# Compressed branch of the decode sequences: two sequences per pass, 256 columns for each weight block

## Chip, core and metric

One core of a Trainium2 chip runs the whole program. The metric is the device time in microseconds of one execution. Engines are named as the profile names them: PE (matmul, with its weight loads as PEld), DVE (vector), ACT (scalar), POOL, and SP, which here only issues DMAs.

## What is computed

One step of a small decoder trunk: a conformer layer (depthwise convolution and a SwiGLU feed-forward) and then a sparse-attention layer, for a prompt of 512 tokens and for 8 decode sequences of 4 tokens with a cache of 1024 tokens each. The part that is changed is the compressed branch of the 8 decode sequences. Each block of 32 cached tokens becomes one key and one value for each of 4 heads, by a two-layer network on the 32*64 = 2048 numbers of the block:

```python
def compress(kv_full, w_phi1, b_phi1, w_phi2, b_phi2, pe_cmp):
    blk = kv_full[:, :n * CMP_BLOCK].reshape(B, n, CMP_BLOCK, 2, KV_HEADS, HEAD_DIM)
    blk = blk + pe_cmp.transpose(1, 0, 2)[:, :, None, :]
    blk = blk.transpose(0, 1, 3, 4, 2, 5).reshape(B, n, 2, KV_HEADS, CMP_BLOCK * HEAD_DIM)
    hid = jax.nn.silu(jnp.einsum('bnegf,efh->bnegh', blk, w_phi1) + b_phi1[:, None, :])
    out = jnp.einsum('bnegh,ehd->bnegd', hid, w_phi2) + b_phi2[:, None, :]
```

A sequence has 32 blocks and 4 heads, so 128 columns for keys (e = 0) and 128 for values (e = 1). The cache is float32 and these products are made in plain float32; `w_phi1` has 16 blocks of 128x128 for each e. The embedding `pe_cmp` is the same for all blocks, so its share is worked out once and added to the bias.

## The kernel before, in words

A scheduler sets the order on each engine: the program is written as nested Python generators, each instruction gets a priority by its place in the code, and inside `tc.high_priority(-LATER)` it gets a lower one, so that it fills places where an engine would wait. The instructions of one engine then run strictly in that order, each waiting for its inputs and for free buffers.

`compress_steps` (lines 1033 to 1071) is such a filler. For each of the 8 sequences b, and for two halves hp, one indirect DMA on POOL (L1030) gathers 1 MB of cache rows into `nat` (2 buffers); DVE transposes it (L1043, two per `nat`) into `xt`, shared by both halves (3 buffers); then for e = 0 and 1 PE multiplies 16 weight blocks `w1`, each 128x128 and stationary, with 128 columns of `xt` into one PSUM bank (L1049). For b = 0 the embedding's share is made between them: the same 16 weight blocks stationary, one column of `peT` moving (L1053), added to the bias on DVE (`bh`, L1055). ACT makes the Silu (`hk`, L1057, 2 buffers), PE the second layer (L1060 for keys, L1066 for values), and DVE adds its bias (`cks`, L1064; `cv`, L1069, one buffer, written to DRAM by L1070). The banks are those of the pool `t`, of which there are two.

The steps are written ahead of the depthwise convolution's end, the layer norm and the second pointwise product of layer 0 (`depthwise`, `layer_norm_out`: L812 are the norm's sums, L818 to L830 its vector work, `h_lo` of L830 its last output, L183 and L185 the large products in fp32r). They are followed by the first feed-forward (`ffn`): eight plain units of gate and up products, of which each ends with one `a_lo` (L920) on POOL, then eight down products, then units with seven half-size products (L247). Beside the feed-forward run the bias tables (L1085 to L1119) and 24 key steps, which gather cache rows (`kr`, L1030), transpose them on DVE (`ktr`, L1304) and write them back to DRAM (L1299, L1307). The bias tables' memory is free only when the compressed branch is done. L452 are the modulation products, a second filler, whose 0.5 MB slabs come through SP's queue with the weights.

Of the kernel before, what the change touches and what calls it, by code (L numbers as in the profile page):

```python
# [7 lines left out]
F32 = mybir.dt.float32  # L8
F32R = mybir.dt.float32r
I32 = mybir.dt.int32  # L10
AF = mybir.ActivationFunctionType
ALU = mybir.AluOpType
AX = mybir.AxisListType

P = 128
# [3 lines left out]
NB = 8  # L19
# [6 lines left out]
G = 4  # L26
R = 4
HD = 64
# [22 lines left out]
STATE = 2  # L51
LAST = KT - 1
ORDER = (0, 1, 2, 3, 4, 5, 6, 7)
MID = 24
PE_CONV = (3, 4, 5, 6, 7)

BUCKET_START = [16, 21, 27, 35, 46, 59, 77, 99, 128, 166, 216, 280, 363, 470, 609, 790]
# [56 lines left out]
class Kernel:  # L114
# [881 lines left out]
    def compress_loads(self, pool):  # L996
        A = self.A

        self.w1 = pool.tile([P, 2, 8, 2, P], F32, name="w1")
        src = A["w_phi1"].rearrange("e (a s h i) n -> e h a i s n", s=8, a=4, h=2)  # L1000
        for e in range(2):
            for h in range(2):
                for a in range(4):
                    self.sy.dma_start(self.w1[32 * a:32 * a + 32, e, :, h], src[e, h, a])
        cp = self.cp
        self.w2k = cp.tile([P, P], F32, name="w2k")
        self.w2v = cp.tile([P, HD], F32, name="w2v")
        for d in range(2):
            self.sy.dma_start(self.w2k[:, d * HD:(d + 1) * HD], A["w_phi2"][0])
        self.sy.dma_start(self.w2v, A["w_phi2"][1])  # L1010
        self.b2k = cp.tile([P, 1], F32, name="b2k")
        b2 = A["b_phi2"][0].rearrange("(d o) -> d o", o=1)
        for d in range(2):
            self.sy.dma_start(self.b2k[d * HD:(d + 1) * HD], b2)
        self.b2v = cp.tile([P, HD], F32, name="b2v")
        self.sy.dma_start(self.b2v, A["b_phi2"][1].rearrange("(o d) -> o d", o=1).broadcast_to([P, HD]))
        self.bh = cp.tile([P, 2], F32, name="bh")
        pe = pool.tile([P, P], F32, name="hk", bufs=2)[:, :HD]
        self.v.memset(pe, 0.0)
        src = A["pe_cmp"].rearrange("e (a s) d -> a e s d", a=4)  # L1020
        for a in range(4):
            for e in range(2):
                self.sy.dma_start(pe[32 * a + 8 * e:32 * a + 8 * e + 8], src[a, e])
        self.peT = pool.tile([P, 2, 32], F32, name="peT")
        self.v.transpose(self.peT, pe.rearrange("p (h i) -> p h i", h=2))
# [6 lines left out]
    def compress_steps(self, pool):  # L1032


        v, s, g, te = self.v, self.s, self.g, self.te
        self.compress_loads(pool)
        for b in range(NB):
            xts = [self.shift_pool.tile([P, 8, 8, 32], F32, name="xt", bufs=3) for _ in range(2)]
            for hp in range(2):
                nat = pool.tile([P, 4, 512], F32, name="nat", bufs=2)  # L1040
                self.load_rows(nat.rearrange("p t e -> p (t e)"), self.A["cache_kv_cmp"], hp, b)
                for e in range(2):
                    v.transpose(xts[e][:, hp * 4:hp * 4 + 4].rearrange("p s q n -> p s (q n)"), nat[:, :, e * 256:(e + 1) * 256])  # L1043
                yield
            for e in range(2):
                xv = xts[e].rearrange("p s (g h) n -> p h s g n", h=2)
                ph = self.bank()
                for c in range(16):
                    te.matmul(ph[:, :P], self.w1[:, e, c // 2, c % 2], xv[:, c % 2, c // 2], start=c == 0, stop=c == 15)  # L1049
                if b == 0:  # L1050
                    pb = self.bank()
                    for c in range(16):
                        te.matmul(pb[:, :1], self.w1[:, e, c // 2, c % 2], self.peT[:, c % 2, e * 8 + c // 2:e * 8 + c // 2 + 1],  # L1053
                                  start=c == 0, stop=c == 15)
                    v.tensor_scalar(self.bh[:, e:e + 1], pb[:, :1], self.b_phi1[:, e:e + 1], None, op0=ALU.add)  # L1055
                hk = pool.tile([P, P], F32, name="hk", bufs=2)
                s.activation(hk, ph[:, :P], AF.Silu, bias=self.bh[:, e:e + 1])  # L1057
                po = self.bank()
                if e == 0:
                    te.matmul(po[:, :P], self.w2k, hk, start=True, stop=True)  # L1060
                    pv = po[:, :P].rearrange("p (q g n) -> p q g n", q=2, g=2)
                    for g2 in range(2):
                        sl = slice(g2 * HD, (g2 + 1) * HD)
                        v.tensor_scalar(self.cks[sl, b], pv[sl, :, g2], self.b2k[sl], None, op0=ALU.add)  # L1064
                else:
                    te.matmul(po[:, :HD], hk, self.w2v, start=True, stop=True)  # L1066
                    cv = pool.tile([32, 256], F32, name="cv", bufs=1)
                    for gg in range(G):
                        v.tensor_tensor(out=cv[:, gg * HD:(gg + 1) * HD], in0=po[gg * 32:(gg + 1) * 32, :HD], in1=self.b2v[:32], op=ALU.add)  # L1069
                    g.dma_start(self.vtail[b, 0:32], cv)  # L1070
            yield
        self.dump("cks", self.cks)

# [572 lines left out]
    def run(self):  # L1646
        tc, A = self.tc, self.A

        def sbuf(name, side="left"):
            return tc.tile_pool(name=name, bufs=1, side=side, reuse_waits="tile")  # L1650

        with sbuf("const") as self.cp, sbuf("norm") as self.np, \
# [17 lines left out]
            with sbuf("conv") as pool:  # L1670
                self.ys0 = pool.tile([P, KT, NS], F32, name="ys0")
                self.conv_pool = pool
                shifting = sbuf("shift", "right")
                self.shift_pool = shifting.__enter__()
                with sbuf("setup", "right") as sp:
                    self.setup(sp)
                    between = self.ada_steps(0, 2)
                    ada1 = itertools.chain(*(self.ada_steps(1, part) for part in (1, 0, 2)))
                    units_ = self.gated_units(pool, between)
                    next(units_)  # L1680
                    self.state_parts(sp)
                compressing = sbuf("compress", "right")
                self.compress_pool = compressing.__enter__()
                next(units_)
                compress = self.compress_steps(self.compress_pool)

                with tc.high_priority(-LATER):
                    for _ in between:
                        pass
                    for _ in range(MID):  # L1690
                        next(compress)
                acc = self.depthwise(pool)
                with tc.high_priority(-LATER):
                    self.conv_states(pool)
                self.layer_norm_out(pool, acc, ada1)
# [119 lines left out]
```

## Time and profile before

| | |
|---|---|
| median of 3 runs (range) | 1661.1 us (1657.52 to 1663.83) |
| profiled execution: time, span of its instructions | 1661.26 us, 1659.5 us |
| busy: PE, DVE, ACT, POOL | 1555.0, 1107.8, 694.1, 235.2 us |
| mean granted clock of TensorE | 0.975 |
| DMA | 295.26 MB, mean 178 GB/s |

The profiled execution's span lies 1.8 us under its own time, and that time 0.2 us over the median. Busy time says little about matmuls, because consecutive ones overlap: what one costs is the distance from its start to the next one's. A float32 matmul shows as two records. The granted clock is given in shares of 2.4 GHz: 1.00 is that level, 0.50 is 1.2 GHz.

### The profile page before, as it was taken

What the parts mean: (1) busy time and instruction counts of PE and PEld (TensorE: products, weight loads), DVE (VectorE), ACT (ScalarE), POOL (GpSimd) and SP (SyncE); (2) the same over time, 40 slices, a digit from 0 to 9 for tenths busy, and PEclk for the clock granted to TensorE, in tenths of its full rate; (3) what the DMA queues carried; (4) which work ended last, traced back from release to release, by engine and by line L of the source; (5) the groups of instructions that cost most, each with busy time, mean ns of one, the idle gap of its engine ahead of it and who ended that gap; (6) DMA issues with size and microseconds to landing.
All of it is one profiled execution on the core that took longest, in us unless ns stands there. A gap on an engine that the chain in (4) does not pass through costs nothing.

```text
span 1659.5 us, 31626 instructions
## 1 busy us (share of the span) xinstructions
PE 1555.0 (94%) x12423; PEld 1366.8 (82%) x12423; DVE 1107.8 (67%) x2369; ACT 694.1 (42%) x1443; POOL 235.2 (14%) x270
## 2 busy tenths in 40 slices
PE   6897998999988889999999899999999999999997
PEld 3784677989978878999977677655699999999997
DVE  2897866482447788576657644867856865874865
ACT  5321115242222344255445422755746542552554
POOL 3444401021220112001110000000011110110010
PEclk9898979999999999999999999999999999999999
DMA  9577575374399999834779895746122472333231
GB/s 307 140 200 155 151 241 168 117 227 130 112 241 312 299 303 325 247 103 106 184 228 306 245 282 183 237 148 229 52 68 73 152 233 84 91 114 90 79 91 64
DMA packets 315568, 295.26 MB, mean 178 GB/s; under 512 B 16019, under 2 KB 275485, under 8 KB 311179
## 3 DMA queue, kind: packets, MB, share of 16 engines
q1 hardware_dynamic: 304507, 237.24, 48.7%
q0 software_dynamic: 10224, 55.47, 10.7%
q8 instruction: 98, 1.61, 0.4%
q10 hardware_dynamic: 688, 0.53, 0.1%
q14 instruction: 51, 0.42, 0.1%
HBM read 256.28 MB, written 45.48 MB: 182 GB/s over the span
## 4 chain that ended last, share of the span: by engine, by line
PE 65%; DMA 13%; DVE 10%; issue 6%; SPq 2%; ACT 2%; POOL 1%; ACTq 0%; DVEq 0%; POOLq 0%
PE g L185 18%; PE g L183 17%; PE g L247 8%; DMA raw<-in_w_down_dram 4%; PE t L247 3%; PE t L155 3%; PE o L1530 2%; DMA raw<-in_w_ada_dram 2%; DVE wlo L196 2%; PE t L1049 2%; PE a L452 1%; PE t L1379 1%; PE t L730 1%; PE sc L1509 1%; DVE y L768 1%
## 5 line engine op out<-in xcount | busy, mean ns | idle before, releaser
L169 ACT CAST whi<-raw 128x512 fp32r<-128x512 f32 x250 | 149.7, 606 | 408.7 <-PE g L185 280.1
L170 DVE TENSOR_TENSOR wlo<-raw,whi 128x512 fp32r<-128x512 f32 x250 | 173.0, 696 | 156.5 <-ACT whi L169 155.6
L183 PE MATMUL g<-h_hi,whi 128*128 128x256 f32 (+1 forms) x584 | 170.5, 293 | 13.9 <-DVE un L680 9.3
L185 PE MATMUL g<-h_hi,whi 128*128 128x288 f32 (+4 forms) x584 | 173.5, 298 | 0.9 <-ACT h_hi L575 0.9
L185 PE MATMUL g<-h_hi,wlo 128*128 128x288 f32 (+4 forms) x584 | 173.9, 298 | 0.0
L185 PE MATMUL g<-h_lo,whi 128*128 128x288 f32 (+4 forms) x584 | 173.7, 297 | 0.0
L183 PE MATMUL g<-h_lo,whi 128*128 128x256 f32 (+1 forms) x584 | 168.3, 288 | 3.0 <-DVE h_lo L830 3.0
L183 PE MATMUL g<-h_hi,wlo 128*128 128x256 f32 (+1 forms) x584 | 167.3, 287 | 0.0
L183 PEld LDWEIGHTS g<-h_hi,whi 128*128 128x128 f32 x584 | 111.5, 191 | 27.3 <-issue 16.2
L247 PE MATMUL g<-T,whi 128*128 128x272 f32 x656 | 127.9, 291 | 4.1 <-DVE sg L261 2.5
L195 ACT CAST whi<-s 128x512 fp32r<-128x512 f32 x128 | 79.1, 620 | 99.9 <-PE g L247 61.7
L183 PE MATMUL g<-a_hi,whi 128*128 128x256 f32 (+1 forms) x372 | 108.0, 291 | 12.4 <-ACT ht L912 4.3
L183 PEld LDWEIGHTS g<-h_lo,whi 128*128 128x128 f32 x584 | 111.8, 192 | 8.0 <-issue 4.3
L185 PEld LDWEIGHTS g<-h_hi,whi 128*128 128x128 f32 x584 | 111.3, 191 | 4.2 <-issue 2.9
L185 PEld LDWEIGHTS g<-h_hi,wlo 128*128 128x128 f32 x584 | 111.3, 191 | 2.6 <-issue 2.5
L185 PEld LDWEIGHTS g<-h_lo,whi 128*128 128x128 f32 x584 | 111.2, 190 | 2.6 <-issue 2.5
L183 PEld LDWEIGHTS g<-h_hi,wlo 128*128 128x128 f32 x584 | 111.5, 191 | 1.8 <-issue 1.7
L196 DVE TENSOR_TENSOR wlo<-s,whi 128x512 fp32r<-128x512 f32 x128 | 89.1, 698 | 34.0 <-ACT whi L195 32.2
L185 PE MATMUL g<-a_hi,wlo 128*128 128x288 f32 (+1 forms) x372 | 111.1, 299 | 0.0
L185 PE MATMUL g<-a_hi,whi 128*128 128x288 f32 (+1 forms) x372 | 110.9, 299 | 0.0
L185 PE MATMUL g<-a_lo,whi 128*128 128x288 f32 (+1 forms) x372 | 110.7, 298 | 0.0
L247 PEld LDWEIGHTS g<-T,whi 128*128 128x128 f32 x656 | 103.8, 190 | 5.6 <-ACT whi L195 2.2
(511 smaller groups left out, 4165.2 us busy)
## 6 DMA issues: line engine op xcount, KB each, us to landing
raw<-in_w_ada_dram SPq DMA_DIRECT2D x84, 512.0 KB
raw<-in_w_gate_dram SPq DMA_DIRECT2D x44, 512.0 KB
raw<-in_w_up_dram SPq DMA_DIRECT2D x44, 512.0 KB
raw<-in_w_down_dram SPq DMA_DIRECT2D x32, 512.0 KB
raw<-in_w_pw_dram SPq DMA_DIRECT2D x24, 512.0 KB
kt_d<-ktr SPq DMA_DIRECT2D x96, 128.0 KB
kt<-kt_d SPq DMA_DIRECT2D x24, 512.0 KB
raw<-in_w_kv_dram SPq DMA_DIRECT2D x20, 512.0 KB
```

What stands on the lines that cost most here:

```text
L155: self.te.transpose(out, in_, self.ident[:n, :n])
L169: self.s.copy(hi[:, :b - a], raw[:, a:b])
L170: self.v.tensor_tensor(out=lo[:, :b - a], in0=raw[:, a:b], in1=hi[:, :b - a].bitcast(F32), op=ALU.subtract)
L183: self.te.matmul(pg[:, 0, :split], a, b[:, i, :split], start=st, stop=sp)
L185: self.te.matmul(pg[:, 1, :tokens - split], a, b[:, i, split:tokens], start=st, stop=sp)
L195: self.s.copy(hi, src)
L196: self.v.tensor_tensor(out=lo, in0=src, in1=hi.bitcast(F32), op=ALU.subtract)
L247: self.te.matmul(out, a[:, i], b(i), start=first and i == 0 and j == 0, stop=i == 3 and j == 2, skip_group_check=not first)
L452: self.te.matmul(pa[32 * j:32 * j + 32, :256], self.cT[:, k, :], w[:, j * 256:(j + 1) * 256], start=k == 0, stop=k == KT - 1)
L730: self.te.matmul(pt[32 * gg:32 * gg + 32], wds[q // 4][:, gg, q % 4], vs[:, gg, 4 * q:4 * q + cols], start=q == 0, stop=q == 7)
L1049: te.matmul(ph[:, :P], self.w1[:, e, c // 2, c % 2], xv[:, c % 2, c // 2], start=c == 0, stop=c == 15)
L1530: te.matmul(po[rp * HD:(rp + 1) * HD, :256], self.vn[:, br, t, gg * HD:(gg + 1) * HD], pT[:, rp * 256:(rp + 1) * 256], start=br == 0 and t ...
```

## The change

`compress_steps` now takes two sequences at a time. For each half hp both `nat` are loaded, each `xt` holds one e of one half for both sequences, and PE multiplies each weight block with 256 columns; the two accumulations of a pair (keys and values) stay open in both banks of `t` over the two halves. `hk` is 256 columns wide and has one buffer. The embedding's share is made first, for both e: the one column of `peT` is stationary and the 128 columns of the weight block move, so the result is a row, which ACT copies and PE turns into a column. All steps are drawn ahead of the depthwise end, as before (24 steps were all there were).

```diff
-        for b in range(NB):
-            xts = [self.shift_pool.tile([P, 8, 8, 32], F32, name="xt", bufs=3) for _ in range(2)]
+        pb = self.bank()
+        for e in range(2):
+            for c in range(16):
+                te.matmul(pb[:1, e * P:(e + 1) * P], self.peT[:, c % 2, e * 8 + c // 2:e * 8 + c // 2 + 1], self.w1[:, e, c // 2, c % 2],
+                          start=c == 0, stop=c == 15)
+        row = pool.tile([P, 2, P], F32, name="hk", bufs=1)[:1]
+        s.copy(row, pb[:1, :2 * P].rearrange("p (e n) -> p e n", e=2))
+        pb = self.bank()
+        for e in range(2):
+            self.transpose(pb[:, e:e + 1], row[:, e])
+        v.tensor_tensor(out=self.bh, in0=pb[:, :2], in1=self.b_phi1, op=ALU.add)
+        yield
+
+        for b in range(0, NB, 2):
+            phs = [self.bank() for _ in range(2)]
             for hp in range(2):
-                nat = pool.tile([P, 4, 512], F32, name="nat", bufs=2)
-                self.load_rows(nat.rearrange("p t e -> p (t e)"), self.A["cache_kv_cmp"], hp, b)
+                nats = [pool.tile([P, 4, 512], F32, name="nat", bufs=2) for _ in range(2)]
+                for i in range(2):
+                    self.load_rows(nats[i].rearrange("p t e -> p (t e)"), self.A["cache_kv_cmp"], hp, b + i)
                 for e in range(2):
-                    v.transpose(xts[e][:, hp * 4:hp * 4 + 4].rearrange("p s q n -> p s (q n)"), nat[:, :, e * 256:(e + 1) * 256])
+                    xt = self.shift_pool.tile([P, 2, 4, 8, 32], F32, name="xt", bufs=3)
+                    for i in range(2):
+                        v.transpose(xt[:, i].rearrange("p s q n -> p s (q n)"), nats[i][:, :, e * 256:(e + 1) * 256])
+                    xv = xt.rearrange("p i s (g h) n -> p s h i g n", h=2)
+                    for c in range(8):
+                        k = 4 * hp + c // 2
+                        te.matmul(phs[e][:, :2 * P], self.w1[:, e, k, c % 2], xv[:, c // 2, c % 2], start=hp == 0 and c == 0, stop=hp == 1 and c == 7)
                 yield
             for e in range(2):
-                xv = xts[e].rearrange("p s (g h) n -> p h s g n", h=2)
-                ph = self.bank()
-                for c in range(16):
-                    te.matmul(ph[:, :P], self.w1[:, e, c // 2, c % 2], xv[:, c % 2, c // 2], start=c == 0, stop=c == 15)
...
-                hk = pool.tile([P, P], F32, name="hk", bufs=2)
-                s.activation(hk, ph[:, :P], AF.Silu, bias=self.bh[:, e:e + 1])
+                hk = pool.tile([P, 2, P], F32, name="hk", bufs=1)
+                s.activation(hk.rearrange("p i n -> p (i n)"), phs[e][:, :2 * P], AF.Silu, bias=self.bh[:, e:e + 1])
```

The scheduler makes a new order from this. All lines of the changed kernel ahead of the change are one lower (L812 is L811 there), those behind it twelve higher. Three places show it.

On PE at the end of the depthwise convolution, where the embedding's share is made (`w_1798` is `w1`), before:

```order
L1053 MATMUL t<-peT,w_1798 128x1 x15
L155 MATMUL b<-c_small,ut 30x128
L452 MATMUL a<-raw,cT 32x256 x4
L155 MATMUL b<-c_small,ut 30x128
L1060 MATMUL t<-hk,w2k 128x128
L1049 MATMUL t<-xt,w_1798 128x128 x13
L452 MATMUL a<-raw,cT 32x256 x4
L1049 MATMUL t<-xt,w_1798 128x128 x3
L1053 MATMUL t<-peT,w_1798 128x1 x12
L812 MATMUL g<-acc,ones 128x272 x2
```

and in the changed kernel, at the same place:

```order
L1040 MATMUL t<-w_1798,peT 1x128 x15
L154 MATMUL b<-c_small,ut 30x128
L451 MATMUL a<-raw,cT 32x256 x4
L154 MATMUL t<-c_small,hk 128x1 x2
L1063 MATMUL t<-xt,w_1798 128x256 x8
L154 MATMUL b<-c_small,ut 30x128
L1063 MATMUL t<-xt,w_1798 128x256 x9
L451 MATMUL a<-raw,cT 32x256 x4
L1063 MATMUL t<-xt,w_1798 128x256 x5
L451 MATMUL a<-raw,cT 32x256 x4
L811 MATMUL g<-acc,ones 128x272 x2
```

The second run of one-column matmuls has moved ahead to the first and has 128 columns now, and 22 matmuls of 256 columns stand where there were 16 of 128.

On DVE in the layer norm, between its reciprocal and the last `h_lo`, the end of that row before:

```order
L463 TENSOR_TENSOR mod<-b,vec 128x2x4x9
L467 TENSOR_SCALAR mod<-mod 128x72
L468 TENSOR_TENSOR mod<-mod,vec 128x72
L1043 STREAM_TRANSPOSE xt<-nat 128x1024 x2
L830 TENSOR_TENSOR h_lo<-ht,h_hi 128x544
L827 TENSOR_TENSOR ht<-y,rstd 128x544
L830 TENSOR_TENSOR h_lo<-ht,h_hi 128x544 x2
```

and in the changed kernel:

```order
L1059 STREAM_TRANSPOSE xt<-nat 128x1024
L467 TENSOR_TENSOR mod<-mod,vec 128x72
L1081 TENSOR_TENSOR cv<-t,b2v 32x64 x4
L1059 STREAM_TRANSPOSE xt<-nat 128x1024 x2
L829 TENSOR_TENSOR h_lo<-ht,h_hi 128x544 x3
L826 TENSOR_TENSOR ht<-y,rstd 128x544 x2
L1059 STREAM_TRANSPOSE xt<-nat 128x1024
L829 TENSOR_TENSOR h_lo<-ht,h_hi 128x544 x2
```

In the whole order 25 of the 32 transposes stand ahead of the last `h_lo`, where it was 18. Between the eight instructions of L818 (L817 in the changed kernel) and the last `h_lo` there are 16, where it was 9. On PE, by the same count, 87 of the 128 matmuls of the first layer stand ahead of the second half of the pointwise product's first pair of outputs, where it was 103 of 256.

On POOL in the first feed-forward, where the key steps' loads begin, before:

```order
L920 TENSOR_TENSOR a_lo<-ht,a_hi 128x544 x3
L1070 DMA vtail<-cv 32x256
L920 TENSOR_TENSOR a_lo<-ht,a_hi 128x544
L1070 DMA vtail<-cv 32x256 x2
L920 TENSOR_TENSOR a_lo<-ht,a_hi 128x544
L1085 DMA ln<-in_c_line_dram 33x1664
...
L920 TENSOR_TENSOR a_lo<-ht,a_hi 128x544
L1119 DMA bs_d<-bs 4x32x394 x2
L1030 DMA kr<-in_cache_kv_sel_dram,rows_78 128x2048 x2
```

and in the changed kernel:

```order
L1082 DMA vtail<-cv 32x256 x2
L1097 DMA ln<-in_c_line_dram 33x1664
...
L919 TENSOR_TENSOR a_lo<-ht,a_hi 128x544 x2
L1109 DMA line_r<-lsb 512x1x320 x2
L1106 DMA line_f<-lsb 16x512 x2
L1131 DMA bs_d<-bs 4x32x394 x2
L1029 DMA kr<-in_cache_kv_sel_dram,rows_78 128x2048 x2
```

The compressed branch is done before the first `a_lo`, and the first key load comes after two of them, not after six. On DVE the eight `cv` additions of a pair stand in two fours; after the first pair four transposes stand between the fours, after the third two. From the first down products of the last third on, the orders of both kernels are the same on all engines.

## Rows read from the trace of the kernel before

**Rows 1.** The page: span by engine, and the granted clock in 40 slices (tenths)

```profile
PE 1555.0 (94%) x12423; PEld 1366.8 (82%) x12423; DVE 1107.8 (67%) x2369; ACT 694.1 (42%) x1443; POOL 235.2 (14%) x270
PEclk9898979999999999999999999999999999999999
```

**Rows 2.** First layer (L1049) and embedding (L1053): forms with counts and ns

```profile
L1049 PE MATMUL t<-xt,w x512: 270/275/527, 207.1 to 435.3; 128*128 128x128 f32 x171
L1053 PE MATMUL t<-peT,w x64: 167/250/352, 213.9 to 241.7; 128*128 128x1 f32 x64
```

**Rows 3.** PE in time: start, length (us), line, count, [idle before, releaser]

```profile
221.74 5.69 PE L1053 MATMUL t<-peT,w 128*128 128x1 f32 x26
230.27 5.21 PE L1049 MATMUL t<-xt,w 128*128 128x128 f32 x26
236.76 2.74 PE L1053 MATMUL t<-peT,w 128*128 128x1 f32 x24
239.36 1.16 PE L812 MATMUL g<-acc,ones 128*128 128x272 f32 x4
254.56 1.08 PE L812 MATMUL g<-sq,ones 128*128 128x272 f32 x4
255.48 0.27 PE L155 MATMUL b<-c_small,ut 128*30 128x128 f32 x1
```

**Rows 4.** Chain that ended last: start, length (us), records of the first layer

```profile
431.99 3.57 PE t L1049 x32
```

**Rows 5.** Stretches: length; busy us (records) by engine; clock; DMA share; GB/s

```profile
221.10:234.80 13.70, 13.01 (x64) 11.69 (x65) 6.97 (x13) 2.31 (x5) 0.94 (x1) 0.50 0.64 197
234.80:267.00 32.20, 30.84 (x243) 24.98 (x242) 19.74 (x29) 13.84 (x24) 3.01 (x4) 1.00 0.57 191
267.00:286.00 19.00, 14.94 (x107) 13.91 (x106) 15.24 (x28) 14.65 (x26) 2.62 (x3) 0.91 0.46 147
286.00:372.00 86.00, 83.38 (x707) 78.50 (x706) 52.09 (x97) 28.09 (x48) 10.63 (x12) 1.00 0.55 168
475.00:550.00 75.00, 64.47 (x484) 60.95 (x483) 50.53 (x91) 17.94 (x34) 8.41 (x8) 0.91 0.98 305
550.00:690.00 140.00, 127.24 (x978) 117.85 (x978) 109.49 (x179) 56.65 (x110) 20.77 (x17) 0.98 1.00 311
```

**Rows 6.** PE in time at its waits in the layer norm

```profile
278.05 0.39 PE L183 MATMUL g<-h_hi,whi 128*128 128x256 f32 x1 [1.03 <-ACT h_hi L829]
281.85 0.39 PE L183 MATMUL g<-h_lo,whi 128*128 128x256 f32 x1 [3.03 <-DVE h_lo L830]
```

**Rows 7.** DVE in order of time: embedding's bias, transposes and h_lo

```profile
227.46 0.22 DVE L1055 TENSOR_SCALAR bh<-t,vec 128x1 f32<-128x1 f32 x1 [7.59 <-PE t L1053]
245.62 1.23 DVE L1043 STREAM_TRANSPOSE xt<-nat 128x1024 f32<-128x1024 f32 x1
279.94 1.25 DVE L1043 STREAM_TRANSPOSE xt<-nat 128x1024 f32<-128x1024 f32 x1 [1.30 <-DMA nat<-in_cache_kv_cmp_dram,rows]
286.41 1.34 DVE L830 TENSOR_TENSOR h_lo<-ht,h_hi 128x544 fp32r<-128x544 f32 x2
```

**Rows 8.** Loads into nat (first) and writes of cv (second): issue to landing

```profile
DMA to landing us min/median/max: 5.6/7.3/10.6
...
DMA to landing us min/median/max: 1.7/1.8/4.2
```

**Rows 9.** POOL in order of time: two a_lo and the first key load

```profile
441.30 1.70 POOL L920 TENSOR_TENSOR a_lo<-ht,a_hi 128x544 fp32r<-128x544 f32 x1 [0.79 <-ACT a_hi L919]
456.29 1.41 POOL L920 TENSOR_TENSOR a_lo<-ht,a_hi 128x544 fp32r<-128x544 f32 x1
473.32 1.05 POOL L1030 DMA_INDIRECT kr<-in_cache_kv_sel_dram,rows  x1 [11.97 <-DMA line_f<-lsb]
```

**Rows 10.** DMA packets: 373 to 445 us first, then 445 to 690

```profile
DMA packets 9272, 8.33 MB, mean 116 GB/s; under 512 B 287, under 2 KB 8479, under 8 KB 9051
...
DMA packets 79342, 71.55 MB, mean 292 GB/s; under 512 B 3544, under 2 KB 74524, under 8 KB 77273
```

More of the change, by code (lines that the diff above doesn't have):

```diff
@@ L53 @@
 ORDER = (0, 1, 2, 3, 4, 5, 6, 7)
-MID = 24
 PE_CONV = (3, 4, 5, 6, 7)
@@ L1017, in compress_loads @@
         self.bh = cp.tile([P, 2], F32, name="bh")
-        pe = pool.tile([P, P], F32, name="hk", bufs=2)[:, :HD]
+        pe = pool.tile([P, 2, P], F32, name="hk", bufs=1)[:, 0, :HD]
         self.v.memset(pe, 0.0)
@@ L1044, in compress_steps @@
                 yield
             for e in range(2):
-                xv = xts[e].rearrange("p s (g h) n -> p h s g n", h=2)
-                ph = self.bank()
-                for c in range(16):
-                    te.matmul(ph[:, :P], self.w1[:, e, c // 2, c % 2], xv[:, c % 2, c // 2], start=c == 0, stop=c == 15)
[L1050 to L1055, printed above, removed]
@@ L1056, in compress_steps @@
-                hk = pool.tile([P, P], F32, name="hk", bufs=2)
-                s.activation(hk, ph[:, :P], AF.Silu, bias=self.bh[:, e:e + 1])
+                hk = pool.tile([P, 2, P], F32, name="hk", bufs=1)
+                s.activation(hk.rearrange("p i n -> p (i n)"), phs[e][:, :2 * P], AF.Silu, bias=self.bh[:, e:e + 1])
                 po = self.bank()
                 if e == 0:
-                    te.matmul(po[:, :P], self.w2k, hk, start=True, stop=True)
-                    pv = po[:, :P].rearrange("p (q g n) -> p q g n", q=2, g=2)
+                    te.matmul(po[:, :2 * P], self.w2k, hk.rearrange("p i n -> p (i n)"), start=True, stop=True)
+                    pv = po[:, :2 * P].rearrange("p (i q g n) -> p i q g n", i=2, q=2, g=2)
@@ L1062, in compress_steps @@
                     for g2 in range(2):
                         sl = slice(g2 * HD, (g2 + 1) * HD)
-                        v.tensor_scalar(self.cks[sl, b], pv[sl, :, g2], self.b2k[sl], None, op0=ALU.add)
+                        v.tensor_scalar(self.cks[sl, b:b + 2], pv[sl, :, :, g2], self.b2k[sl], None, op0=ALU.add)
                 else:
[L1066 to L1069, printed above, removed]
@@ L1070, in compress_steps @@
-                    g.dma_start(self.vtail[b, 0:32], cv)
+                    for i in range(2):
+                        te.matmul(po[:, i * HD:(i + 1) * HD], hk[:, i], self.w2v, start=True, stop=True)
+                    for i in range(2):
+                        cv = pool.tile([32, 256], F32, name="cv", bufs=1)
+                        for gg in range(G):
+                            v.tensor_tensor(out=cv[:, gg * HD:(gg + 1) * HD], in0=po[gg * 32:(gg + 1) * 32, i * HD:(i + 1) * HD], in1=self.b2v[:32], op=ALU.add)
+                        g.dma_start(self.vtail[b + i, 0:32], cv)
@@ L1689, in run @@
                         pass
-                    for _ in range(MID):
-                        next(compress)
+                    for _ in compress:
+                        pass
                 acc = self.depthwise(pool)
```

## The prediction

> **What bounds the kernel now.** The page comes first. PE is busy for 94% of the span, and the clock row has digits under 9 only among the first six of its 40 slices [rows 1]. So the end is set by PE's stream, and a change counts where it shortens the stream, fills its waits or raises its clock. The lines that are changed come next: 512 records of the first layer and 64 of the embedding [rows 2]. A float32 matmul shows as two records, so these are 256 and 32 matmuls. Their last column gives overlapping durations, and a cost has to be read from starts. Then I read the stretches by time [rows 5]. The compressed branch lies in 207 to 435 us, and PE's losses there are: idle 0.69 us in 221 to 235, 1.36 to 267, 4.06 to 286 and 2.62 to 372, together 8.7 us; and 221.1 to 234.8 wholly at half clock, with 13.01 us of it busy. In 267 to 286 the clock is 0.91, so 0.18 of 19 us or 3.4 us are at half, which costs 1.7. Behind the branch is the stage of the key steps: in 475 to 690 PE is idle for 10.5 + 12.8 = 23.3 us, and clocks of 0.91 and 0.98 mean 13.5 and 5.6 us at half, a loss of 9.6 us; together 33 us, with DMA at 0.98 to 1.00 [rows 5].
>
> **A. First layer, same arithmetic in half as many matmuls.** Before: 32 records of a stream that nothing interrupts take 3.57 us, so 111 ns each [rows 4], and 512 of them 56.8 us. After: 256 records of 256 columns, a form that the trace lacks. The nearest row is L812 with 272 columns: 4 records from 254.56 to 255.48, 230 ns each [rows 3]. Columns therefore set the pace, and 256 cost 230 x 256/272 = 216 ns at most; the straight line from 128 to 272 columns (111 to 230) gives 217. Twice 108 would be 215, which I take as the lower side: 256 x 0.215 = 55.0. **A = -1.8 us**, bounds 0 and -1.8. The second layer's products do the same columns, and Silu and the `cks` additions the same elements with fewer instructions off the path: 0.
>
> **B. Embedding.** Before, 24 records of one column go from 236.76 to 239.36: 108 ns each at full clock [rows 3]. After, 128 columns move, 111 ns. 64 x 0.003 = 0.2, and two small transposes 0.1. **B = +0.3**, bounds 0 and +1. ACT's row copy and the transposes lengthen the path to `bh`, but PE has the 22 first-layer matmuls of the first pair behind it as cover (22 x 0.43 = 9.5 us). Without that cover the first Silu would be some 1 us late.
>
> **C. The clock where the embedding stood.** In 221.74 to 227.4 PE ran 26 one-column records at 5.69/26 = 219 ns, twice 108, and the level came back only when a run of 128-column records had begun at 230.27 [rows 3, 5]. DVE waited 7.59 us for the result [rows 7]. After, no long run of one-column matmuls is left; each embedding matmul has 128 columns, and 22 wide ones follow. If the run of one-column records is why the level fell, all of 13.01 us halves: -6.5. If the level falls for another reason but returns as it did here, 4.5 us behind the start of a wide stream (230.27 to 234.8), 9.2 of 13.7 us are at full level, worth at most -4.3. A second run of one-column records at 236.76 kept the full level [rows 3], so the cause isn't certain, and I take the smaller gain. **C = -4.3**, bounds 0 and -6.5.
>
> **D. PE's waits between 207 and 372 us.** Before they are the 8.7 us and the 1.7 for the clock; the two that can be named are 1.03 us for `h_hi` and 3.03 us for the last `h_lo` but two [rows 6]. DVE is late there since it waits for `nat` by 1.30 us and does transposes first [rows 7]. The new order puts 16 transposes between L817 and the last `h_lo`, against 9: 7 x 1.23 = 8.6 us more of DVE. PE has more to do meanwhile: 16 transposes feed 64 matmuls of 0.43 us, 27.5 us, where 9 fed 72 of 0.222, 16.0 us. That is 11.5 us more cover against 8.6 of work, so the named waits mostly go; I keep 1.0 and the 1.7. New waits arise since both banks of `t` are held by an open pair. The next pair's second accumulation waits for eight `cv` additions, and in DVE's order four transposes stand between the fours. Four additions take 0.9 us (estimate from the 0.22 us of the small DVE row), four transposes 4.9, four additions 0.9: 6.7 us, of which eight matmuls of keys hide 3.4: 3.3 us. The second `cv` tile's write also needs 1.8 us [rows 8], hidden behind the transposes. At the second boundary the norm's products stand between: 0. At the third, two transposes and feed-forward vector work: 2.7. New: 3.3 + 2.7 + 1.7 + 1.0 = 8.7 against 10.4. **D = -1.7**; bounds -10.4 (all filled) and +9 (nothing filled, new waits on top with their clock).
>
> **E. Key steps earlier.** The first key load stands at 473.32 [rows 9] behind six `a_lo`; now it is behind two. Units are 456.29 - 441.30 = 15.0 us apart [rows 9], so it may come some 60 us earlier. DMA moved 8.33 MB in 373 to 445 at 116 GB/s and 71.55 MB in 445 to 690 at 292 [rows 10]: there is room ahead. Spread over 305 us, the same bytes and 6.9 MB that lie there already need 257 GB/s, 12% less than 292. If the 33 us of loss shrink by that share: **E = -4.0**. Bounds: the loss of the later stretch alone, 12.8 + 2.8 = 15.6, vanishes; or nothing shrinks and the 60 us ahead lose at its rate, 60 x 15.6/140 = +6.7.
>
> **Sum.** -1.8 + 0.3 - 4.3 - 1.7 - 4.0 = -11.5 us. Against the profiled execution, 1661.3 us (its span is 1659.5, and it stands 0.2 over the median), that is 1649.8: **1650 us**, with A and C at 0 it is 1656, with C at -6.5 and E at -11 it is 1640: the forecast's own range.
>
> **Rivals.** **Clean:** the cover fills all of D, the level never falls, E takes half its bound: -1.8 + 0.3 - 6.5 - 10.4 - 7.8 = -26.2, so 1635. For it speaks that the transposes no longer wait behind `bh`; against it, the new order holds both banks.
>
> **Waits only move:** the level falls for another reason, new waits equal old, and the key steps meet the same full queue later (DMA at 0.98 to 1.00 [rows 5]). A and B stay: 1660. For it speaks the second one-column run at full level.
>
> **Loads in pairs bind DVE (slower):** a group is now two loads and four transposes, and both buffers come free only at its end. At the median landing of 7.3 us [rows 8] four groups, the first one loaded ahead, need 4.9 + 3 x (7.3 + 4.9) = 41.5 us from 245.62. The last `h_lo` came at 286.41, 40.8 us later [rows 7], and PE has 11.5 us more to do in between: 52.3. It decides from a landing of 10.9 us; the longest before is 10.6. If two loads issued together are served one after the other, 14.6, the chain is 63.4: +11.1, and three waits of that size bring a half clock of 1.7 each, +5.1. With A, B and C -5.8: 1672. Against it: two loads were in flight before too, and DVE waited for them 1.30 us at most in the rows shown. Beside this, the row of C shows a level that falls in a stretch with hardly an idle microsecond. The Trainium skill, page "TensorE: Matmul & The Clock Gate", section "A second HAM failure mode: psum-queue depth-cycling", says that a kernel whose matmul groups cycle through PSUM banks idles briefly between groups and its clock then oscillates. That speaks against this change, which holds both banks; it would put such losses at the three pair boundaries of D, and no row of before shows it.
>
> **Weight loads set the pace:** a record of one column costs 108 ns and one of 128 costs 111 [rows 3, 4], as if the stationary operand's load were the price. Then 256 columns would cost 111 as well: 256 x 0.111 = 28.4, -28.4 in place of -1.8, and 1623. The 230 ns of L812 [rows 3] speak against it. The same page, section "Back-to-back issue gap", gives about 81 ns for 128 columns and 131 for 512, by which wider matmuls are cheap; the float32 rows here differ from it.
>
> **How the numbers follow.** Forecast 0.50, clean 0.12, waits only move 0.21, loads bind 0.15, weight pace 0.02. The range 1635 to 1667 leaves out the last two. 0.5%, about what a measurement of this kernel can tell, is 8.3 us: faster is below 1652.8, slower above 1669.4. The forecast's own range lies below 1652.8 for 0.7 of its chance: faster 0.12 + 0.02 + 0.35 = 0.49; same 0.21 + 0.15 = 0.36; slower 0.15.
>
> **What the new profile would show.** A: a pitch near 215 ns per record of L1063 at full clock. C: no slice at half clock behind L1040; a stretch of 10 us at 0.50 there would refute it. D: PE's waits for `h_lo` under 1 us, and two for `cv` of some 3 us. E: the first `kr` near 415 us and less idle PE in 475 to 690. The sum is wrong above all if the level falls elsewhere, if `nat` lands later than 10.9 us, or if the key steps' loss merely starts earlier.

## The result, and the profile after

| | before | changed |
|---|---|---|
| median (range) of the runs beside each other | 1660.9 us (1657.5 to 1663.8) | 1639.9 us (1636.9 to 1651.3) |
| ratio, 95% interval | | 0.9884 (0.984 to 0.9928) |
| the same comparison again, 5 more runs (`e1_after`) | 1662.2 us | 1640.5 us, 0.9862 (0.9834 to 0.9891) |

The change makes the kernel some 21 us faster, and the intervals exclude 1: inside the range of the prediction (1635 to 1667), but nearly twice the forecast sum of 11.5 us.

The first profile of the changed kernel caught its longest run (1651.3 us). The second one, `e1_after`, took 1640.5 us, the median, so the rows below are from it. Of the kernel before a second trace was taken too, `e9_before` (1663.8 us). The page of `e1_after`, busy time and granted clock, against [rows 1]:

```profile
PE 1543.3 (94%) x12161; PEld 1348.6 (82%) x12161; DVE 1106.1 (67%) x2360; ACT 692.7 (42%) x1436; POOL 238.3 (15%) x270
PEclk8898999999899999999999999999999999999999
```

PE's share is the same 94%, with 12 us less busy than before. Slice 6, which had 7 before, is at 9; slice 1, ahead of the changed code, has gone from 9 to 8. The page says little more; the stages do. Below are five of them, of the second trace of before and then of the changed kernel. They are cut at the same work in both: the last but one `acc` addition of the convolution on DVE, L818, the last `h_lo`, the first `a_lo`, the eighth `a_lo`, and a residual addition behind the down products. Columns as in [rows 5].

```profile
207.00:240.40 33.40, 30.15 (x233) 24.26 (x232) 20.45 (x40) 2.78 (x6) 3.20 (x3) 0.74 0.76 264
240.40:288.00 47.60, 42.38 (x303) 36.05 (x302) 34.69 (x57) 28.78 (x49) 7.49 (x8) 0.90 0.48 162
288.00:375.40 87.40, 84.75 (x716) 79.38 (x716) 52.31 (x97) 28.38 (x48) 10.28 (x12) 0.99 0.54 170
375.40:494.70 119.30, 115.99 (x932) 110.58 (x931) 47.31 (x85) 31.02 (x56) 22.20 (x28) 0.99 0.56 155
494.70:693.20 198.50, 179.16 (x1374) 167.17 (x1378) 150.42 (x254) 69.56 (x135) 26.07 (x22) 0.97 1.00 310
```

```profile
210.00:242.30 32.30, 28.93 (x236) 20.07 (x228) 19.90 (x38) 1.62 (x5) 3.21 (x3) 0.90 0.74 255
242.30:295.50 53.20, 51.19 (x298) 42.42 (x297) 42.26 (x66) 30.64 (x50) 12.89 (x13) 1.00 0.66 229
295.50:380.50 85.00, 83.61 (x631) 75.58 (x630) 53.83 (x108) 28.13 (x46) 10.88 (x17) 1.00 0.49 155
380.50:484.80 104.30, 96.39 (x753) 90.88 (x752) 49.15 (x73) 28.40 (x51) 20.24 (x22) 0.95 0.93 265
484.80:673.30 188.50, 178.38 (x1394) 167.43 (x1393) 138.50 (x241) 70.22 (x135) 23.04 (x18) 0.97 0.86 270
```

Three things are to be seen. The **front**, up to the first `a_lo`, is about as long as before: 168.4 us, then 170.5. The **later part**, up to the common residual, is 25 us shorter: 317.8, then 292.8. And in the front PE loses much less. I call loss what a stage has of idle time (length minus busy) and of clock (one minus the clock, times the length); the first row gives 33.4 - 30.15 + 0.26 x 33.4 = 11.9. Summed over the front the loss falls from 25.4 to 10.0 us; over the later part it stays, 29.8 and 28.9. (The first traces of both kernels give 21.5 and 9.8, then 32.8 and 34.4.)

How a front of the same length with less loss shortens what follows is told by the first layer's records in the front and in the stage behind it, first L1049 of `e9_before`, then L1063 of `e1_after`:

```profile
207.00:375.40 168.40, 51.58 (x370) 48.08 (x368) 0.92 0.57 186
375.40:494.70 119.30, 18.38 (x143) 17.39 (x142) 0.99 0.56 155
...
210.00:380.50 170.50, 58.48 (x256) 47.49 (x256) 0.98 0.59 197
380.50:484.80 104.30, 0.00 (x0) 0.00 (x0) 0.95 0.93 265
```

Before, 143 of the 512 records came after the first `a_lo` (one lies across the cut and is counted on both sides) and stood in the feed-forward. Now none do.

### The profile page after: what moved, and what is told of

The parts are those of the page before. It is cut to its first block, busy times and chain, and to the rows that moved or that the text cites. A ratio compares the mean times of both kernels' runs of the same rounds, so it can differ in the third digit from the quotient of the medians.

```text
span 1649.5 us, 31082 instructions
## 1 busy us (share of the span) xinstructions
PE 1545.9 (94%) x12161; PEld 1349.5 (82%) x12161; DVE 1105.8 (67%) x2360; ACT 692.6 (42%) x1436; POOL 237.5 (14%) x270
## 3 DMA queue, kind: packets, MB, share of 16 engines
q0 software_dynamic: 10224, 55.47, 10.6%
## 4 chain that ended last, share of the span: by engine, by line
PE 66%; DMA 13%; DVE 10%; issue 6%; ACT 2%; POOL 1%; SPq 1%; ACTq 0%; DVEq 0%; POOLq 0%
PE g L184 18%; PE g L182 17%; PE g L246 11%; PE t L246 4%; PE t L154 3%; PE o L1542 3%; DMA raw<-in_w_ada_dram 2%; DVE wlo L195 2%; DMA nat<-in_cache_kv_cmp_dram,rows 2%; DVE y L767 2%; DMA raw<-in_w_down_dram 1%; DMA raw<-in_w_gate_dram 1%; PE t L1391 1%; PE t L729 1%; DMA bs<-bs_d 1%
```

## The experiments

The five stages were cut at the same work in every kernel. `late` is the number of `a_lo` ahead of the first key load in POOL's order. Losses and lengths are of one trace each, which repeats to some 4 us between the two traces of before and to some 6 between those of the changed kernel; ratios are of the timed runs. The kernel before was timed beside each set of runs, with a median of 1662.2 us beside `e1_after` to `e4_keylate`, 1662.4 beside `e5_colfirst` to `e8_split128` and 1659.0 beside `e9_before` to `e12_thinbefore`, so across these sets the ratios are to be compared, not the medians.

| kernel | ratio to before (95%) | median us | late | front: length, loss | later: length, loss |
|---|---|---|---|---|---|
| `e9_before` | 1.0006 (0.9983 to 1.0028) | 1662.5 | 6 | 168.4, 25.4 | 317.8, 29.8 |
| `e1_after` | 0.9862 (0.9834 to 0.9891) | 1640.5 | 2 | 170.5, 10.0 | 292.8, 28.9 |
| `e2_row` | 0.9931 (0.9908 to 0.9955) | 1649.8 | 6 | 169.7, 19.2 | 307.1, 30.5 |
| `e3_col` | 0.987 (0.9841 to 0.9899) | 1639.9 | 2 | 172.5, 12.4 | 293.0, 27.7 |
| `e4_keylate` | 0.9937 (0.9907 to 0.9966) | 1649.8 | 5 | 170.7, 9.3 | 303.6, 41.2 |
| `e5_colfirst` | 0.9953 (0.9931 to 0.9974) | 1653.1 | 6 | 167.0, 15.9 | 303.2, 20.1 |
| `e6_keylater` | 0.9953 (0.9936 to 0.9971) | 1652.5 | 8 | 170.2, 9.0 | 293.0, 32.9 |
| `e7_keysfirst` | 0.9882 (0.9855 to 0.991) | 1642.7 | 1 | 174.5, 16.9 | 286.2, 20.0 |
| `e8_split128` | 0.9963 (0.994 to 0.9985) | 1654.9 | 5 | 164.3, 12.6 | 316.5, 39.6 |
| `e10_thin` | 0.9867 (0.9831 to 0.9903) | 1640.8 | 1 | 167.3, 55.4 | 298.0, 28.3 |
| `e11_key2` | 0.9956 (0.9928 to 0.9984) | 1654.2 | 3 | 172.3, 11.3 | 301.2, 34.8 |
| `e12_thinbefore` | 0.9843 (0.9807 to 0.9879) | 1639.5 | 1 | 170.3, 54.3 | 288.5, 21.4 |

The traced run of `e5_colfirst` was its fastest (1645.8 us against a median of 1653.1), so its later part reads too short. That of `e4_keylate` took 1657.6 us against a median of 1649.8, so its later part and the loss there read too long. `e6_keylater` and `e7_keysfirst` push other work past the last cut (the next stage is 11 us longer than in `e1_after`), so their later parts can't be compared; their ratios can.

### The two traces again, and the two halves of the change

`e1_after` is the changed kernel:

> The changed kernel once more, for a second trace and a tighter interval. Theory 1 (clock and waits): the gain lies between 207 and 375 us, from less half clock at the embedding and fewer PE waits; from the first a_lo to 692 us PE's idle time plus clock loss stays within 3 us of the 31.8 us of before. Theory 2 (the prediction's term E): that later stage loses at least 4 us less than before. Both expect about 1640 us.

The time repeats. The gain does lie in the front's losses, as theory 1 said, and the later loss is within 1 us of before, which speaks against theory 2 as it was put. The next runs show that this isn't the whole of it.

`e9_before` is the kernel before:

> The kernel before, unchanged, for a second trace of it and as a measure of the scatter: ratio 1.00. If the accounts by stage hold, its losses (idle time plus clock) are 18 to 24 us between 207 and 373 us and 28 to 35 us from the first a_lo to 692 us. Rival (the first trace was an outlier): losses near those of the changed kernel, 10 and 25 us.

The first trace of before was no outlier: 25.4 us in the front, just above the 18 to 24 that were expected, and 29.8 in the later part.

`e2_row` makes only the embedding's share in the new way, with the loop of before behind it (here and in `e5_colfirst` one more step is drawn ahead, since the embedding is a step of its own):

```diff
+        pb = self.bank()
+        for e in range(2):
+            for c in range(16):
+                te.matmul(pb[:1, e * P:(e + 1) * P], self.peT[...], self.w1[...], start=c == 0, stop=c == 15)
...
         for b in range(NB):
-                if b == 0:
-                    pb = self.bank()
...
```

> The kernel before with only the embedding changed: its column stationary and 128 columns of the weight block moving, made ahead of the loop; sequences still one by one with 128 columns. Theory 1: the half clock of 221 to 235 us goes, worth 4 to 6 us, the rest of the gain stays out: about 1655 us. Rival (the gain comes from the two-sequence loop alone): 1661 us. Rival (the embedding is all of it): 1640 us.

`e3_col` is the other half: two sequences at a time, but the embedding with one column moving.

```diff
-                te.matmul(pb[:1, e * P:(e + 1) * P], self.peT[...], self.w1[...], start=c == 0, stop=c == 15)
+                te.matmul(pb[:, e:e + 1], self.w1[...], self.peT[...], start=c == 0, stop=c == 15)
```

> The changed kernel with the embedding made as before, the 128x128 weight block stationary and one column moving, at the place where the changed kernel has it. Theory 1: the 32 one-column matmuls bring a half clock back, 4 to 6 us over the changed kernel: about 1645 us. Rival (the clock fell for another reason than the one-column matmuls): no half clock beyond 4 us there, 1640 us.

The loop alone gives the whole gain (0.987), the embedding alone half of it (0.9931), both together no more than the loop (0.9862). Half clock is back in `e3_col`, for 13.6 us at a stretch, as these rows show (the first is that stretch alone, the second the stage that contains most of it):

```profile
207.60:221.20 13.60, 13.60 (x86) 9.50 (x88) 9.85 (x22) 0.00 (x0) 1.96 (x2) 0.50 0.88 324
208.30:237.40 29.10, 29.10 (x204) 21.00 (x204) 18.84 (x36) 0.85 (x2) 3.20 (x3) 0.72 0.64 213
```

and costs nothing that the runs can tell (1639.9 us against 1640.5; the front of its one trace is 2 us longer than in `e1_after`). PE is never idle in that stage. Here is what it does at its start in `e3_col`, and then in `e1_after`, where PE stands still in the same stage for one transfer:

```profile
207.55 0.58 PE L729 MATMUL g<-xt,sq 128*32 128x256 f32 x1 [2.06 <-DMA xt<-up]
208.56 3.15 PE L1040 MATMUL t<-peT,w 128*128 128x1 f32 x14
...
209.70 0.61 PE L729 MATMUL g<-xt,sq 128*32 128x256 f32 x1 [2.33 <-DVE xt L1059]
210.53 2.52 PE L1040 MATMUL t<-w,peT 128*1 128x128 f32 x11
213.11 1.25 PE L1040 MATMUL t<-w,peT 128*1 128x128 f32 x10
219.36 0.40 PE L451 MATMUL a<-raw,cT 128*32 128x256 f32 x1 [3.37 <-DMA raw<-in_w_ada_dram]
```

At half clock PE takes longer over work that it would otherwise finish and wait behind. Theory 1's clock term fell. The rival of `e3_col` had the time right and its sign wrong, since there is more half clock than 4 us. Yet the one-column matmuls didn't bring it there: the level was at 0.50 from 207.6 us on, behind a wait of 2.06 us and 1 us ahead of the first of them. It falls at the same place in `e1_after`, behind a wait of 2.33 us, and is back some 3.3 us later (11 records of 128 columns take 2.52 us, then 10 take 1.25). What differs is how long it lasted, 13.6 us with one column moving. Nor do such records always run slowly: 30 of them from 224.06 us on took 3.51 us in `e3_col`, 117 ns each.

`e5_colfirst` tells place from form in the loop of before: both e's one-column matmuls ahead of the loop.

```diff
+        pb = self.bank()
+        for e in range(2):
+            for c in range(16):
+                te.matmul(pb[:, e:e + 1], self.w1[...], self.peT[...], start=c == 0, stop=c == 15)
...
         for b in range(NB):
-                if b == 0:
...
```

> The kernel before with the embedding still as one-column matmuls, but made ahead of the loop for both e at once, as the row form was in e2_row (1649.8 us). Theory 1 (the place gives that gain: the bias is ready earlier and the branch ends sooner; the clock that one-column matmuls cost is taken from waits): about 1650 us. Theory 2 (the form gives it, through the clock): half clock of some 14 us stays near 210 us, and the time is about 1656 us or more.

1653.1 us lies between the two, and its interval overlaps that of `e2_row`. With 0.9953 most of `e2_row`'s gain is there without the new form; a remainder of some 4 us for the form (0.0022, and more within the intervals) isn't excluded in this loop. Half clock was there as well, from 209.8 to 216.5 us and from 223.6 to 230.3, and here it did begin among one-column matmuls with PE at work.

### What lies under the first layer's matmuls

`e10_thin` leaves out three quarters of the first layer's product:

```diff
-                    for c in range(8):
+                    for c in (0, 7):
                         k = 4 * hp + c // 2
```

> The changed kernel with 32 of the 128 matmuls of the first layer (two of each eight), which leaves out three quarters of that product: 96 x 0.43 = 41 us less of PE. Theory (the wide matmuls cover waits for DVE and DMA in the depthwise end and the norm): 10 us or more of waiting comes to light there, and the time is 1608 us or more. Rival (PE's stream alone sets the time, nothing is covered): 1599 us.

41 us less of PE, and a ratio of 0.9867 in place of 0.9862, with an interval of 6 us to either side. Its front, cut in the same way:

```profile
209.60:242.00 32.40, 26.60 (x231) 16.43 (x226) 22.80 (x45) 8.04 (x19) 3.75 (x4) 0.90 0.81 286
242.00:295.90 53.90, 38.08 (x195) 29.63 (x196) 44.56 (x64) 25.00 (x38) 15.45 (x14) 0.78 0.71 233
295.90:376.90 81.00, 71.27 (x536) 63.70 (x536) 51.53 (x110) 28.94 (x49) 8.57 (x15) 0.89 0.50 152
```

The second stage takes 53.9 us against 53.2, though PE is busy for 38.1 instead of 51.2 and at a clock of 0.78. So something other than PE's work is as long there. DVE is busy for 44.6 us, and waits for loads; its waits in that stage, `e1_after` first, then `e10_thin` (total us, times, longest):

```profile
DVE xt L1059 <- DMA nat<-in_cache_kv_cmp_dram,rows: 11.6, 6, 3.3
...
DVE xt L1059 <- DMA nat<-in_cache_kv_cmp_dram,rows: 8.4, 4, 3.2
```

Busy time and waits for `nat` fill DVE's stage in both. The chain that ended last in `e10_thin` runs through the same loads, of which three in that stage are:

```profile
253.97 7.99 DMA nat<-in_cache_kv_cmp_dram,rows
...
268.10 7.19 DMA nat<-in_cache_kv_cmp_dram,rows
...
283.69 7.01 DMA nat<-in_cache_kv_cmp_dram,rows
```

In `e1_after` the chain of that stage runs through PE instead: the wide matmuls of L1063 are 46.3% of it, and no load into `nat` is in it. So two chains of nearly the same length stand side by side there, and taking work out of one of them bares the other. And not all of the 41 us was saved: in the front PE was busy for 28 us less (136.0 against 163.7), while the loss to the clock rose from 3.2 to 24.0 us.

`e12_thinbefore` does the same to the kernel before:

```diff
-                for c in range(16):
+                for c in (0, 5, 10, 15):
                     te.matmul(ph[:, :P], ...)
```

> The kernel before with 64 of the 256 matmuls of the first layer (four of each sixteen), three quarters of that product left out: 192 x 0.222 = 43 us less of PE. The branch then ends sooner and the first key load comes after one a_lo, as early as in the changed kernel. Theory (one sequence at a time leaves the norm's waits and the early key steps give 9 us): about 10 us over e10_thin. Rival (the loop matters only through the end of the branch, so through the key steps): equal to e10_thin within 3 us.

The rival holds: 1639.5 us, as `e10_thin` beside it. With little product to place, both loops end by the first `a_lo`, both have their first key load behind one `a_lo`, both fronts take 167 to 170 us, and nothing of the change is left. What the change alters is how much of the product has been done by then, and with it how early the key steps begin. Here too the clock took much of what was left out: 36 of the 54.3 us of loss in the front are clock.

### The key steps

`e4_keylate` holds the bias tables and the key steps back:

```diff
                     shifting.__exit__(None, None, None)
+                    for _ in range(8):
+                        yield
                     with sbuf("bias") as pool2:
```

> The changed kernel with the bias tables and the key steps held back by four plain units, so that the first key load comes after five a_lo instead of two, as late as before the change. Theory 1: no change against the changed kernel, within 3 us of 1640. Theory 2 (term E): the 4 to 8 us that the earlier key steps gave are lost, 1644 to 1648 us.

Theory 2 was right here: 9 us, a little over its 4 to 8. The front is that of the changed kernel; the two stages of the later part are, in a run 8 us over the median,

```profile
378.50:481.80 103.30, 94.84 (x736) 90.23 (x734) 39.48 (x62) 28.02 (x49) 17.25 (x17) 0.96 0.65 174
481.80:682.10 200.30, 183.75 (x1378) 170.06 (x1378) 148.68 (x252) 70.23 (x136) 26.28 (x21) 0.94 0.92 292
```

against DMA shares of 0.93 and 0.86 in `e1_after`. PE's longest group of waits in the last stage, for split weights, is three times that of `e1_after` (first `e4_keylate`, then `e1_after`):

```profile
PE g L246 <- DVE wlo L195: 9.4, 6, 3.3
...
PE g L246 <- DVE wlo L195: 3.1, 1, 3.1
```

`e11_key2` and `e6_keylater` have 4 and 16 in place of 8 in that line; `e7_keysfirst` puts the bias tables behind the key steps:

```diff
-                    with sbuf("bias") as pool2:
-                        self.bias_tables(pool2)
-                        yield
                     with sbuf("keys") as pool2:
...
+                    with sbuf("bias") as pool2:
+                        self.bias_tables(pool2)
+                        yield
```

> The changed kernel with bias tables and key steps held back by two plain units, the first key load after three a_lo. The delays measured so far: none 1640.5, four units 1649.8, eight units 1652.5 us. Theory E (the cost grows with the delay until the loads all lie behind the plain units): 1643 to 1648 us. Rival (a step between two and five a_lo, from a collision with one transfer): 1640 or 1650 us.

> The changed kernel with the bias tables and the key steps held back by eight plain units instead of four, so that the first key load comes after all eight a_lo, later than before the change. Theory E (each unit of delay squeezes the key steps' loads into a shorter stage): another 5 to 10 us over e4_keylate (1649.8), so 1655 to 1660 us. Rival (four units of delay only met one bad collision): 1650 us or less.

> The changed kernel with the bias tables behind the key steps instead of ahead of them, so that the first key load comes after one a_lo and waits for no bias table. Theory E: the loads begin some 20 us earlier than in the changed kernel, worth 3 to 8 us: 1632 to 1637 us; the PE wait of 6.7 us at 419 us, behind a key load that came late on the queue, goes too. Rival (the gain of an early start is used up, or the bias tables now collide with the last key loads and weights): 1640 us or more.

The cost doesn't grow with the delay. One or two `a_lo` ahead of the first key load give 0.9882 and 0.9862; three, five and eight give 0.9956, 0.9937 and 0.9953, which the intervals don't tell apart. The expectations of theory E for `e6_keylater` (another 5 to 10 us), `e7_keysfirst` (3 to 8 us faster) and `e11_key2` (1643 to 1648 us) all failed, and the rival of `e11_key2` held in kind: a step between two and three, though the time lies 4 us above its 1650 and no collision was seen. What stands at that step wasn't found; `e11_key2`'s first key load was issued 10 us after that of `e1_after`:

```profile
417.07 1.06 POOL L1029 DMA_INDIRECT kr<-in_cache_kv_sel_dram,rows  x1 [18.24 <-issue]
...
426.82 1.06 POOL L1029 DMA_INDIRECT kr<-in_cache_kv_sel_dram,rows  x1 [17.27 <-DMA line_f<-lsb]
```

### 256 columns or 128

`e8_split128` keeps the new loop, but splits 14 of each 16 matmuls into two of 128 columns:

```diff
-                        te.matmul(phs[e][:, :2 * P], self.w1[...], xv[:, c // 2, c % 2], ...)
+                        for i in range(2):
+                            te.matmul(phs[e][:, i * P:(i + 1) * P], self.w1[...], xv[:, c // 2, c % 2, i], start=False, stop=False)
```

> The changed kernel with two sequences at a time, but 14 of each 16 matmuls of the first layer split into two of 128 columns with the same weight block. The scheduler then places the bias tables behind four a_lo and the first key load behind five, as in e4_keylate. Theory A (columns set the pace) with E: the matmuls themselves cost 1 to 3 us, the late key steps 9: about 1651 us. Rival (256 columns save weight loading time on PE, over 10 us): 1660 us or more. Rival (key steps don't matter): 1642 us.

1654.9 us; the ratio 0.9963 is to be compared with `e4_keylate`'s 0.9937, whose key steps stand equally late: 4 us or so, within the two intervals, so A is small, as was expected. Most of the 256 columns' worth in this kernel is not the matmul but the order that the scheduler makes of it, with the branch out of the way by the first `a_lo` (in `e8_split128` 48 records still stand behind it).

## Why the prediction was right, and where its steps weren't

**The direction and the range** held. The measured 1640 lies at the lower edge of the forecast's own range (1640 to 1656). The range held by its width more than by the sum: C had its number for another reason, D was several times its term, and E's two parts cancelled in the loss. The rival "clean" (1635, with a chance of 0.12) had the better picture of the front: behind the first stage most of the loss went.

**A (-1.8)** was right in its price. The 32 records of an uninterrupted stream in `e1_after`, and what follows them:

```profile
267.79 7.07 PE L1063 MATMUL t<-xt,w 128*128 128x256 f32 x32
274.70 0.59 PE L1070 MATMUL t<-hk,w2k 128*128 128x256 f32 x2
```

(274.70 - 267.79)/32 = 216 ns, where 215 was taken and 111 is the pitch (the distance from one start to the next) at 128 columns [rows 4]. The rival "weight loads set the pace" is out. The Trainium skill's figures (page "TensorE: Matmul & The Clock Gate", section "Back-to-back issue gap": about 81 ns at 128 columns, 131 at 512) don't describe these float32 matmuls: the measured pitch doubles from 128 to 256 columns.

**B (+0.3)** had no time of its own that the runs can tell: with the loop the new form is worth nothing (`e3_col`).

**C (-4.3)** came out in its number and failed in its reason. The loss of the first stage fell from 11.9 to 6.6 us, 5.3 us. But `e3_col` has the half clock and the time of the changed kernel. The step that failed is "worth at most -4.3": the clock was priced as if PE's stream alone set the end there. It didn't; behind the slow matmuls lay a wait for a transfer, 3.4 us in `e1_after`, which the slow clock merely covers. The sign that was given (no slice at half clock behind L1040) held in part: the long stretch is gone, but two pieces of some 3.3 us, from 209.5 and from 219.8 us, are there.

**D (-1.7)** was mis-sized. In the two stages behind the first one the loss fell from 10.0 + 3.5 to 2.0 + 1.4 us, that is by 10 (by 6 between the first traces: 7.3 + 2.6 to 2.5 + 1.2). The cover argument was right: the wide matmuls fill the norm's waits. What failed are the new waits that were set against it: the 3.3 and 2.7 us for the `cv` additions at the boundaries of pairs didn't come. PE waits in the norm's stage of `e1_after` for one thing only, and in the rest of the front for no `cv` either:

```profile
PE a L451 <- DMA raw<-in_w_ada_dram: 2.0, 1, 2.0
```

The rule of the Trainium skill that spoke against the change ("A second HAM failure mode: psum-queue depth-cycling", the same page) has no case here: with both banks held, the clock of that stage is 1.00, where it was 0.90 (0.96 in the first trace).

**The slower rival** had its mechanism right in part. Loads do hold up DVE: waits for `nat` in the norm's stage went from 2.8 us in `e9_before` to 11.6, and the stage is 5.6 us longer. That the pairs are the reason isn't shown: before, 14 of the 16 loads were issued within 2.3 us of another one too, and the stage now has 16 transposes to feed, where it had 9. The price was wrong: no landing reached 14.6 us (the longest was 12.3), and PE had enough to do to fill the longer stage, busy for 51.2 of 53.2 us. `e10_thin` shows how much hangs on that: without that work PE loses 27.7 us in the same stage (53.9 - 38.08, and 0.22 x 53.9 of clock).

**E (-4.0)** was the wrong sum of two larger things. Against before, the later loss is unchanged (means of two traces 31.3 and 31.7 us). But the branch's matmuls, 143 records of which had stood among its waits, are gone from it, and with late key steps the time is 9 us longer and the loss higher (41.2 us in a run above the median, 34.8 in `e11_key2`, traced at its median). So early key steps save some 9 us, more than twice the term, and the lost cover gives some of that back; how much wasn't measured by itself. `e2_row` speaks for such a cover: 74 records stand behind its first `a_lo`, its key steps come after as many `a_lo` as before, and it is as fast as `e4_keylate`, which has none. The prediction put a price on the DMA's crowding alone and didn't ask what the branch had covered in that stage. Its proportional rule (loss shrinks with the mean rate) failed as well: the times show a step, no slope.

**The sum.** Read from the five stages, which are 22.9 us shorter, the gain is: in the front 25.4 - 10.0 = 15.4 us of loss turned into work (11.7 between the first traces), 0.9 us less loss behind it, about 2 of A, and some 5 us that weren't told apart (the scatter of single traces is as large). That work is the rest of the branch, which no longer stands in the feed-forward: 143 records at 111 ns are 15.9 us. The largest error in number is D. The premise that PE's stream sets the end in the front was half of it: the gain can be read from PE's losses, but `e10_thin` took 41 us of PE work out and the kernel got no faster, partly because the loads' chain is as long in the norm's stage and partly because the clock fell.

**Left open.** What stands between two and three `a_lo`; and why the embedding ahead of the loop of before gives 8 to 12 us (part is front loss, 25.4 to 19.2 and 15.9 us; the rest is in the later part and wasn't told apart). A shorter front wasn't tried, by a third `nat` buffer or by transposes behind the `h_lo`. By `e10_thin` less PE work alone gives nothing there; and since PE is busy for 163.7 of the 170.5 us in `e1_after`, earlier loads alone can give back no more than its 10.0 us of loss. No kernel here beats the changed one clearly: `e3_col` and `e7_keysfirst` are equal to it within their intervals.

## What to carry to other kernels

A filler stream that keeps an engine at 94% busy can hide a second chain of the same length: before pricing its instructions, take most of it out and see whether the time moves, and look at the clock too, which fell with the work here. Where the time doesn't move, fewer of the filler's instructions save nothing there, and its worth is how much of it is done before the stage ends. The remainder stands in the next stage, less what it covers there. In this kernel a half clock in such a stage cost no more than the wait behind it, and work that moved forward took its cover away from the place that it left.

## What the runs showed of the hardware

- Float32 matmuls against a 128x128 weight block cost 111 ns per record at 128 columns, 216 at 256 (`e1_after`) and 230 at 272, two records each, all at full clock; at one column it was 108 ns [rows 3, 4]. So one column cost as much as 128 did, and twice the columns cost nearly twice the time.
- The level fell behind a wait of 2.06 us in `e3_col` and of 2.33 us in `e1_after`; it stayed at 0.50 for 13.6 us where one-column matmuls followed, and for some 3.3 us where 128 columns moved. In `e5_colfirst` it fell at 209.8 us among one-column records that had run at full level from 206.52 us on, with no wait of PE since 205.95. A busy PE was thus no guard against the lower level in this kernel.
- Gathers of 1 MB, nearly all issued in pairs, landed within 12.3 us at most, with a median of 7.7, in `e1_after`, and within 10.6 us, with medians of 6.8 and 7.3, in the two traces of before [rows 8].
